# A two-layer decoder trunk in float32 on one core: second products of Strassen pairs accumulated in PSUM, FoX probabilities normalised at the output's gate

## The chip, the core and the metric

The kernel runs on one core of one Trainium2 chip. TensorE (PE) multiplies matrices into PSUM; VectorE (DVE), ScalarE (ACT) and GpSimd (POOL) work element by element; SyncE (SP) issues most loads. The engines run side by side and wait for one another through semaphores. The metric is the device time of one execution in microseconds (us); lower is better.

## What is computed

A decoder trunk of two layers for 1024 tokens of 1024 features, all in float32. In each layer one projection of the normalised input `h` feeds three branches: forgetting attention (FoX, 8 heads of 64), differential attention (4 heads) and a short gated convolution. Each branch is multiplied by its own SiLU gate and projected back, and the three are merged by sigmoid gates. Cut to what matters here:

```python
h = _rmsnorm(x, pre_g)
p = h @ w_in
(fq, fk, fv, ff, fg, dq, dk, dv, dg, cb, cc, cx, cg, mg) = _split_cols(p)
...
    logits = logits + c[:, :, s0:s1, None] - c[:, :, None, :s1]
    p = jax.nn.softmax(jnp.where(_causal_mask(s0, s1), logits, -jnp.inf), axis=-1)
    outs.append(jnp.einsum('bhqk,bhkd->bhqd', p.astype(v.dtype), v[:, :, :s1]))
...
y_fox = y_fox * jax.nn.silu(fg)
y_diff = y_diff * jax.nn.silu(dg)
y_conv = cb * _short_conv(cc * cx, conv_w)
y_conv = y_conv * jax.nn.silu(cg)
gates = jax.nn.sigmoid(mg + b_m).reshape(b, s, N_BRANCH, D_MODEL)
m = (gates[:, :, 0] * (y_fox @ w_fox)
     + gates[:, :, 1] * (y_diff @ w_diff)
     + gates[:, :, 2] * (y_conv @ w_conv))
return x + _rmsnorm(m @ w_o, post_g)
```

## The kernel before

**Split operands.** A float32 operand is held as two float32r tiles, hi and lo, and a product is lo·hi + hi·lo + hi·hi. `mm3` (L343) issues these three matmuls for each tile of 128 along the summed dimension, at L351, L352 and L353; each goes over 512 columns.

**Strassen pairs.** Two chunks of 128 columns of `w_in` that are used one after the other make a pair, 20 pairs in a layer: 6 for the convolution branch (`conv_pair`), 4 for the merge of that branch (`conv_merge`, where each result is multiplied by one more product, `z`), and 10 for gates that are spilled to DRAM (`gates_spilled`). `strassen` (L483) makes a pair with seven products of 12 matmuls where the plain way takes eight. The weights stand on the left: b11, b21 and b22 are quadrants, t1 to t4 sums of them; on the right stand quadrants of `h` (a11, a12, a22) and sums of them (s1 to s4, made once per layer in `build_s`, L444 to L450). The products come in the order b11·a11, b21·a12, t2·s2, t3·s3, t1·s1, t4·a22, b22·s4, each in a PSUM bank of its own; `bank()` hands the eight banks out in turn. DVE adds them up in SBUF tiles `u` and `v` (L497, L498, L500) and in `total` (L521); `use` takes each of the four results on. In the names of the trace a PSUM bank is S, T, O or F.

**Weights of a pair.** `emit_pair` (L304) makes the split weights of the next pair while PE is at the current one. Two loads bring `wraw`. `put` casts a part to `whi` on ACT (L318) and makes `wlo` on POOL (L319); `sub` (L321) forms t1 to t4 on DVE. The parts lie in four tiles: x (b11, b21), y (t2, t3), z (t1, t4) and b (b22). The pool `ws` has three buffers for each kind of tile, so b takes the buffers that x of the same pair had, x of the next pair those of y, y those of z, and z those of b: the first cast into z waits until the last matmul of b22·s4 is done. The sums t1 to t4 are built in tiles `sw`, of which there are two: t4 overwrites t2, and t3 takes t1's when POOL has read that.

**FoX.** `fox_unit` (L866) works on two blocks of 128 queries of one head at a time. Stage 1 makes negated logits and, in `softmax` (L839), the probabilities: least value per row (L847, DVE), exponential with its row sum (L854, ACT), and `norm`, which takes the reciprocal of the sum (L857) and multiplies the whole row of up to 1024 keys by it (L858, DVE). Stage 2 transposes the probabilities on PE (L174), splits them into `pt` (ACT L821, DVE L822) and multiplies with the values (L893, L894). Stage 1 runs one unit ahead of stage 2. Of each step the program says when it would be due by the class `Clock`, an estimate of PE's time, and `later` puts it into its engine's queue in that order; `need(*done)` puts in what a stage needs before it goes on. Projections of the differential branch are spread between the units; POOL splits their weight tiles at L279.

**Gate of the output.** `y_prep` (L1028) loads the spilled output `o` and its gate `g` for 128 rows, multiplies them (L1038, DVE) and splits the product into `yf` (ACT L1043, POOL L1044). For FoX it runs beside the third of the four differential heads.

Of the kernel before, what the change touches and what calls it, by code (L numbers as in the profile page):

```python
# [11 lines left out]
F32 = mybir.dt.float32  # L12
# [8 lines left out]
S = 1024  # L21
D = 1024
P = 128
# [11 lines left out]
# order of the query blocks (pairs) of a head, and of the FoX heads (pairs)  # L35
G_ORDER = (1, 2, 3, 0)
FOX_ORDER = (2, 3, 0, 1)
# work on the tensor engine that runs beside each attention pair or head
# [12 lines left out]
# weights of the attention's steps when work beside it is spread between them  # L51
W1F, W2F, W1D, W2D = 0.188, 1.324, 0.31, 1.574
# PSUM banks: logits, transposes, outputs, work beside the attention
# [3 lines left out]
def mm_us(n):  # L57
    """Time of a pass of n columns through the tensor engine."""
    return max(n, 128) * 0.000417


class Clock:
    """Estimated time of the tensor engine. What the other engines do after one of its steps is emitted
    when its turn would come, beside later steps, so that no engine's queue waits on an early entry."""
# [57 lines left out]
def interleave(main, main_cost, fill, fill_cost):  # L122
    """Emit the steps of main with those of fill spread evenly between them."""
# [12 lines left out]
class Trunk:  # L136
# [35 lines left out]
    def transpose(self, out, x):  # L172
        """One block of 128 x 128, through the tensor engine."""
        self.nc.tensor.transpose(out, x, self.ident)  # L174
# [88 lines left out]
    def emit_load(self, key, kt, nco, eng):  # L263
        """DMA one weight tile [P, kt*nco] and split it into hi + lo float32r parts."""
# [18 lines left out]
    def load_w(self, key, kt, nco, eng="gpsimd"):  # L283
        """The next weight tile; the loads of the tiles after it are issued ahead of its use."""
# [19 lines left out]
    def emit_pair(self, l, i0, i1):  # L304
        """DMA two 128-column weight chunks, b1j and b2j their upper and lower halves, and form the split
        operands of a Strassen-Winograd step: b11, b21 | b12 - b11 (t1), b21 - t2 (t4) |
        b22 - t1 (t2), b22 - b12 (t3) | b22."""
# [38 lines left out]
    def mm3(self, ps, pairs, start=True, stop=True):  # L346
        """Accumulate the products of split operands: lo*hi + hi*lo + hi*hi for each k tile."""
        nc = self.nc
        n = len(pairs)
        for i, (wh, wl, xh, xl) in enumerate(pairs):  # L350
            nc.tensor.matmul(ps, wl, xh, start=start and i == 0, stop=False)  # L351
            nc.tensor.matmul(ps, wh, xl, start=False, stop=False)  # L352
            nc.tensor.matmul(ps, wh, xh, start=False, stop=stop and i == n - 1)  # L353

    def proj_g(self, w, h):
        """One 128-column chunk of the input projection, transposed, for token half h."""
# [18 lines left out]
    # ------------------------------------------------------------------ norm  # L375
    def rstd(self, ss, scale):
        """(ss * scale + EPS) ** -0.5 per partition."""
# [9 lines left out]
    def hk(self, h, k, o=0, n=512):  # L387
        """Tokens o..o+n of a half of hT, 128-row tile k: hi and lo."""
        return [t[:, k % 2, o:o + n] for t in self.hT[h][k // 2]]

    def norm_rows(self, xs, gB, hT, tb0, step):
        """rmsnorm of blocks of 128 tokens (rows of the tiles xs), transposed and split into hT."""
# [40 lines left out]
    # ------------------------------------------------------------------ Strassen-Winograd  # L433
    def build_s(self, L):
        """Sums of the quadrants of h (tokens x features), split: s1 = a21 + a22, s2 = s1 - a11,
        s3 = a11 - a21, s4 = a12 - s2. a21 itself waits in DRAM meanwhile."""
# [46 lines left out]
    def strassen(self, L, c0, c1, use, uv=None):  # L483
        """Two chunks of the input projection, transposed, with seven products in place of eight.
        use(j, h, x, ps, own): chunk j, token half h is x + ps; x may be overwritten if own."""
# [3 lines left out]
        def product(b, a):  # L489
            ps = self.bank()  # L490
# [821 lines left out]
```

## Time and profile before

| | us |
|---|---|
| median of 3 runs | 2570.14 |
| lowest, highest | 2569.18, 2570.54 |
| span of the profiled execution | 2573.8 |
| PE busy (share of the span) | 2439.4 (95%) |
| DVE busy | 1699.8 (66%) |
| ACT busy | 1109.0 (43%) |
| POOL busy | 838.9 (33%) |

The stages of the two layers lie as follows, in us from the start of the span: convolution pairs and the first two gate pairs 72 to 254 and 1351 to 1534, merge of the convolution to 376 and 1656, gate pairs to 531 and 1812, FoX 585 to 849 and 1865 to 2129, differential attention to 1112 and 2393, then the projections of the branches and the output. A busy time is the sum over the engine's instructions; matmuls are pipelined and overlap in the records, so PE's busy time is an upper reading of its work. "Idle before <- releaser" behind an instruction is the time its engine stood idle ahead of it and what it waited for last.

### The profile page before, as it was taken

To read this page: it belongs to the slowest core of one execution; us is meant where nothing else is said; L and a number is where in the kernel's file an instruction comes from. 1 tells how busy PE (TensorE), PEld (TensorE's weight loads), DVE (VectorE), ACT (ScalarE), POOL (GpSimd) and SP (SyncE) were. 2 spreads that over 40 slices of the span, in tenths; PEclk is the share of its full clock that TensorE was granted. 3 is DMA by queue.
4 is the path that set the end of the run, shared out by engine and by line. 5 is a ranking of instruction groups with operands and counts; after the bars stand their busy time and mean duration, and the time that the engine had idled before them with its cause. 6 is when DMAs were issued, how large, how long until landed. Compare 5 with 4: busy or idle time off the path is not lost. (4 is left out here: it accounts for less than half of the span.)

```text
span 2573.8 us, 35788 instructions
## 1 busy us (share of the span) xinstructions
PE 2439.4 (95%) x13104; PEld 2051.8 (80%) x13104; DVE 1699.8 (66%) x3017; ACT 1109.0 (43%) x2282; POOL 838.9 (33%) x605
## 2 busy tenths in 40 slices
PE   7899999999999999899997999999999999989998
PEld 6677888888978778778976778888888787877798
DVE  6976464447687777767578654344486878777664
ACT  4224333336554554543433232233365545555333
POOL 1566334421112222361025652344211122232600
PEclk9899999999999999999998999999999999999999
DMA  4012223332222222563521122233321222225534
GB/s 167 33 50 95 92 96 111 107 132 70 63 69 68 63 87 64 169 220 129 194 90 41 50 95 89 75 117 130 93 80 53 69 68 75 82 70 186 202 119 180
DMA packets 111808, 260.35 MB, mean 101 GB/s; under 512 B 15744, under 2 KB 40576, under 8 KB 111632
## 3 DMA queue, kind: packets, MB, share of 16 engines
q1 hardware_dynamic: 56304, 183.33, 20.7%
q10 hardware_dynamic: 55328, 74.73, 9.4%
q8 instruction: 104, 1.70, 0.3%
q14 instruction: 72, 0.59, 0.1%
HBM read 183.48 MB, written 55.64 MB: 93 GB/s over the span
## 5 line engine op out<-in xcount | busy, mean ns | idle before, releaser
L279 POOL TENSOR_TENSOR wlo<-wraw,whi 128x1024 fp32r<-128x1024 f32 (+2 forms) x93 | 198.5, 2135 | 628.1 <-ACT whi L276 442.3
L351 PE MATMUL F<-ht,wlo 128*128 128x512 f32 x792 | 331.1, 418 | 0.0
L353 PE MATMUL F<-ht,whi 128*128 128x512 f32 x792 | 318.5, 402 | 0.0
L352 PE MATMUL F<-ht,whi 128*128 128x512 f32 x792 | 317.0, 400 | 0.0
L319 POOL TENSOR_TENSOR wlo<-sw,whi 128x512 fp32r<-128x512 f32 x160 | 224.6, 1414 | 228.6 <-ACT whi L318 203.1
L319 POOL TENSOR_TENSOR wlo<-wraw,whi 128x1024 fp32r<-128x1024 f32 x80 | 159.3, 1992 | 188.1 <-ACT whi L318 187.9
L318 ACT CAST whi<-sw 128x512 fp32r<-128x512 f32 x160 | 96.1, 619 | 245.6 <-DVE sw L321 106.1
L353 PEld LDWEIGHTS F<-ht,whi 128*128 128x128 f32 x792 | 150.8, 190 | 30.6
L276 ACT CAST whi<-wraw 128x1024 fp32r<-128x1024 f32 (+2 forms) x126 | 118.0, 939 | 129.8 <-PE F L353 41.9
L822 DVE TENSOR_TENSOR pt<-T,pt 128x512 fp32r<-128x512 f32 (+1 forms) x240 | 147.4, 632 | 37.4 <-ACT pt L821 35.7
L351 PEld LDWEIGHTS F<-ht,wlo 128*128 128x128 f32 x792 | 152.3, 192 | 24.2
L352 PEld LDWEIGHTS F<-ht,whi 128*128 128x128 f32 x792 | 151.5, 191 | 24.5
L821 ACT CAST pt<-T 128x512 fp32r<-128x512 f32 (+1 forms) x240 | 125.1, 544 | 91.3 <-PE T L174 66.1
L783 PE MATMUL S<-qk,qk 128*128 128x512 f32 (+2 forms) x384 | 141.7, 369 | 23.0 <-ACT p L922 21.1
L174 PE MATMUL T<-ident,p 128*128 128x128 f32 x864 | 135.3, 277 | 11.5 <-DVE p L858 6.6
L922 ACT ACTIVATE p<-S,sm 128x512 f32<-128x512 f32 (+2 forms) x192 | 110.5, 582 | 70.2 <-DVE sm L918 35.4
L916 DVE TENSOR_REDUCE sm<-S 128x1 f32<-128x512 f32 (+2 forms) x192 | 104.5, 551 | 48.5 <-PE S L787 29.6
L784 PE MATMUL S<-qk,sw 128*128 128x512 f32 (+2 forms) x384 | 131.8, 348 | 0.0
L318 ACT CAST whi<-wraw 128x1024 fp32r<-128x1024 f32 x80 | 66.8, 834 | 146.0 <-PE S L353 43.7
L351 PE MATMUL F<-whi,ht 128*128 128x256 f32 (+1 forms) x416 | 121.9, 293 | 4.2 <-DVE vd L373 4.2
L854 ACT ACTIVATE p<-p,sm 128x384 f32<-128x384 f32 (+7 forms) x128 | 99.5, 777 | 54.9 <-DVE sm L847 41.5
L321 DVE TENSOR_TENSOR sw<-wraw,sw 128x512 f32<-128x512 f32 x80 | 69.1, 863 | 81.3 <-POOL wlo L319 80.7
(390 smaller groups left out, 7249.2 us busy)
## 6 DMA issues: line engine op xcount, KB each, us to landing
wraw<-wt SPq DMA_DIRECT2D x128, 512.0 KB
mg<-tmp ACTq DMA_DIRECT2D x64, 256.0 KB
sw<-qk ACTq DMA_DIRECT2D x256, 64.0 KB
g<-mg SPq DMA_DIRECT2D x32, 512.0 KB
wraw<-wo SPq DMA_DIRECT2D x32, 512.0 KB
x<-x SPq DMA_DIRECT2D x24, 512.0 KB
wraw<-wbr SPq DMA_DIRECT2D x48, 256.0 KB
m<-tmp ACTq DMA_DIRECT2D x32, 256.0 KB
```

What stands on the lines that cost most here:

```text
L174: self.nc.tensor.transpose(out, x, self.ident)
L276: nc.scalar.copy(hi, raw)
L279: getattr(nc, eng).tensor_tensor(out=lo, in0=raw, in1=hi.bitcast(F32), op=ALU.subtract)
L318: nc.scalar.copy(w[0][:, o], f)
L319: nc.gpsimd.tensor_tensor(out=w[1][:, o], in0=f, in1=w[0][:, o].bitcast(F32), op=ALU.subtract)
L351: nc.tensor.matmul(ps, wl, xh, start=start and i == 0, stop=False)
L352: nc.tensor.matmul(ps, wh, xl, start=False, stop=False)
L353: nc.tensor.matmul(ps, wh, xh, start=False, stop=stop and i == n - 1)
L783: nc.tensor.matmul(ps[:, :wp], q[:, i * P:(i + 1) * P], k[:, c0:c0 + wp], start=True, stop=False)
L784: nc.tensor.matmul(ps[:, :wp], qsw[:, (i % 2) * P:(i % 2) * P + P], k[:, c0:c0 + wp], start=False, stop=not last)
L821: self.clock.later(0.1, lambda: nc.scalar.copy(hi, T[:, n0:]))
L822: done = self.clock.later(0.6, lambda: nc.vector.tensor_tensor(out=lo, in0=T[:, n0:], in1=hi.bitcast(F32), op=ALU.subtract))
```

## The change

`mm3` gets a flag that lets a product add to a bank that is already in use. In `strassen` the second product of three results goes into the bank of an earlier one: b21·a12 is added to b11·a11, t4·a22 to t3·s3, and b22·s4 to t1·s1. For that the earlier sums must have been read first, so the order of the products becomes b11·a11, t2·s2, t3·s3, t1·s1, b21·a12, t4·a22, b22·s4. Two of DVE's additions go in each pair; `use(0, 0, ...)` now takes the bank itself. A pair takes four PSUM banks in place of seven. The number of matmuls is the same.

In FoX, `norm` keeps only the reciprocal, which goes into a column of the tile `rl` of the head pair; the rows of exponentials stay as they are, and stage 2 needs `exp` in place of `norm`. When the last unit of a head pair is out, `sums_out` transposes `rl` on PE and spills it to `rs` in DRAM. `y_prep` loads each head's reciprocals, broadcast to its 64 rows, into `rb` and multiplies `o` by it on POOL, ahead of the multiplication with the gate: 16 such multiplications of 128x512, and 16 loads.

```diff
-    def mm3(self, ps, pairs, start=True, stop=True):
+    def mm3(self, ps, pairs, start=True, stop=True, more=False):
...
-            nc.tensor.matmul(ps, wl, xh, start=start and i == 0, stop=False)
-            nc.tensor.matmul(ps, wh, xl, start=False, stop=False)
-            nc.tensor.matmul(ps, wh, xh, start=False, stop=stop and i == n - 1)
+            nc.tensor.matmul(ps, wl, xh, start=start and i == 0, stop=False, skip_group_check=more)
+            nc.tensor.matmul(ps, wh, xl, start=False, stop=False, skip_group_check=more)
+            nc.tensor.matmul(ps, wh, xh, start=False, stop=stop and i == n - 1, skip_group_check=more)
...
-        def product(b, a):
-            ps = self.bank()
-            self.mm3(ps, [(w[b][0][:, k], w[b][1][:, k], *(t[:, k % 2] for t in L.a[a][k // 2])) for k in range(4)])
+        def product(b, a, ps=None):
+            more = ps is not None
+            ps = ps or self.bank()
+            self.mm3(ps, [(w[b][0][:, k], w[b][1][:, k], *(t[:, k % 2] for t in L.a[a][k // 2])) for k in range(4)],
+                     not more, True, True)
             return ps

         u, v = uv or (self.tmp(), self.tmp())
-        nc.scalar.copy(u, product("b11", "a11"))
-        use(0, 0, u, product("b21", "a12"), False)
-        nc.vector.tensor_tensor(out=u, in0=u, in1=product("t2", "s2"), op=ALU.add)
-        nc.vector.tensor_tensor(out=v, in0=u, in1=product("t3", "s3"), op=ALU.add)
+        add = lambda o, x, ps: nc.vector.tensor_tensor(out=o, in0=x, in1=ps, op=ALU.add)
+        p1 = product("b11", "a11")
+        nc.scalar.copy(u, p1)
+        p6 = product("t2", "s2")
+        add(u, u, p6)
+        p7 = product("t3", "s3")
+        add(v, u, p7)
         p5 = product("t1", "s1")
-        nc.vector.tensor_tensor(out=u, in0=u, in1=p5, op=ALU.add)
-        use(1, 1, v, p5, False)
-        use(0, 1, v, product("t4", "a22"), True)
-        use(1, 0, u, product("b22", "s4"), True)
+        use(0, 0, None, product("b21", "a12", p1), False)
+        use(1, 1, v, p5, True)
+        use(0, 1, u, product("t4", "a22", p7), False)
+        use(1, 0, u, product("b22", "s4", p5), True)
...
         def norm():
-            nc.vector.reciprocal(out=st[:, 2:3], in_=st[:, 2:3])
-            nc.vector.tensor_scalar(out=pr[:, :n], in0=pr[:, :n], scalar1=st[:, 2:3], scalar2=None, op0=ALU.mult)
+            nc.vector.reciprocal(out=rl, in_=st[:, 2:3])
...
-        later(t, exp)
-        done.append(later(2 * t + 0.2, norm))
+        done.append(later(t, exp))
+        later(2 * t + 0.2, norm)
...
+            if g == G_ORDER[-1] and e == 1:
+                self.clock.later(0.5, lambda: self.sums_out(L, p))
...
+    def sums_out(self, L, p):
+
+        nc = self.nc
+        T = self.pT()
+        self.transpose(T[0:16, 0:P], L.rl[p])
+        r = self.tmp((P, P))
+        nc.scalar.copy(r[0:16], T[0:16, 0:P])
+        nc.scalar.dma_start(L.rs[16 * p:16 * p + 16], r[0:16])
...
+        if kind == "f":
+            rb = self.blk([P, S], F32, "rb")
+            rows = L.rs.rearrange("(h t) q -> h (t q)", t=8)
+            for e in range(2):
+                nc.sync.dma_start(rb[e * 64:e * 64 + 64], rows[2 * c + e:2 * c + e + 1].to_broadcast([64, S]))
...
+            if kind == "f":
+                nc.gpsimd.tensor_tensor(out=o1, in0=o1, in1=rb[:, h * 512:h * 512 + 512], op=ALU.mult)
```

PE's queue, from the last matmuls of b11·a11 of a gate pair on (the same pair in both; `ht_6` and `ht_7` are parts of a12, `s2` those of s2). Before:

```order
L352 MATMUL S_504_2878<-ht_5_110,whi_467_2707 128x512
L353 MATMUL S_504_2878<-ht_4_109,whi_467_2707 128x512
L351 MATMUL T_505_2892<-ht_6_111,wlo_468_2708 128x512
L352 MATMUL T_505_2892<-ht_7_112,whi_467_2707 128x512
L353 MATMUL T_505_2892<-ht_6_111,whi_467_2707 128x512
```

After:

```order
L353 MATMUL T_460_2810<-ht_5_110,whi_426_2644 128x512
L354 MATMUL T_460_2810<-ht_4_109,whi_426_2644 128x512
L352 MATMUL F_461_2824<-s2_99_535,wlo_431_2653 128x512
L353 MATMUL F_461_2824<-s2_100_536,whi_430_2652 128x512
L354 MATMUL F_461_2824<-s2_99_535,whi_430_2652 128x512
```

b21·a12 stood right behind b11·a11, in a bank of its own; now t2·s2 stands there. Where it went is the end of t1·s1 of the same pair (`s1` are parts of s1), after:

```order
L352 MATMUL S_463_2852<-s1_112_570,wlo_433_2657 128x512
L353 MATMUL S_463_2852<-s1_113_571,whi_432_2656 128x512
L354 MATMUL S_463_2852<-s1_112_570,whi_432_2656 128x512
L352 MATMUL T_460_2810<-ht_6_111,wlo_427_2645 128x512
L353 MATMUL T_460_2810<-ht_7_112,whi_426_2644 128x512
```

It goes into `T_460`, the bank of b11·a11, as the fifth product, and t3·s3 has moved from fourth to third.

DVE's queue in FoX, in the first window, from a row's least value (L847 before, L856 after, ISA) to the copy of transposed probabilities. Before:

```order
L847 ISA p_970_5712,sm_972_5718<-S_971_5713,cB_968_5705 128x384
L847 ISA sm_972_5718 128x1
L857 RECIPROCAL sm_966_5697<-sm_966_5697 128x1
L858 TENSOR_SCALAR p_959_5659<-p_959_5659,sm_966_5697 128x256
L857 RECIPROCAL sm_972_5718<-sm_972_5718 128x1
L858 TENSOR_SCALAR p_970_5712<-p_970_5712,sm_972_5718 128x384
L822 TENSOR_TENSOR pt_975_5745<-T_976_5746,pt_975_5745 128x384
```

After:

```order
L856 ISA p_910_5586,sm_912_5592<-S_911_5587,cB_908_5579 128x384
L856 ISA sm_912_5592 128x1
L866 RECIPROCAL rl_759_4749<-sm_905_5570 128x1
L866 RECIPROCAL rl_907_5578<-sm_912_5592 128x1
L830 TENSOR_TENSOR pt_915_5617<-T_916_5618,pt_915_5617 128x384
L856 ISA p_910_5586,sm_918_5641<-S_917_5637,cB_908_5579 128x512
```

The two multiplications of whole rows that stood ahead of the copy are gone, and the reciprocals stay.

## Rows read from the trace of the kernel before

**Rows 1.** The page: busy time of each engine over the span, share, instructions.

```profile
PE 2439.4 (95%) x13104; PEld 2051.8 (80%) x13104; DVE 1699.8 (66%) x3017; ACT 1109.0 (43%) x2282; POOL 838.9 (33%) x605
```

**Rows 2.** Windows: length, busy PE, PEld, DVE, ACT, POOL; PEclk; DMA share; GB/s.

```profile
585.00:849.00 264.00, 252.85 (x1635) 218.11 (x1634) 202.67 (x508) 146.26 (x322) 45.70 (x52) 0.99 0.24 67
1865.00:2129.00 264.00, 251.88 (x1632) 217.54 (x1631) 203.68 (x508) 145.93 (x322) 45.10 (x52) 0.99 0.23 67
395.00:512.00 117.00, 117.00 (x506) 94.96 (x505) 51.56 (x69) 43.76 (x66) 54.11 (x36) 1.00 0.32 108
1500.60:1505.90 5.30, 5.23 (x12) 4.13 (x13) 2.58 (x4) 2.19 (x3) 2.82 (x3) 0.50 0.13 49
```

**Rows 3.** PE's waits: line waited for, us in total, times, longest.

```profile
PE O L893 <- DVE pt L822: 12.6, 8, 2.0
PE O L351 <- POOL wlo L319: 8.6, 1, 8.6
PE T L174 <- DVE p L858: 6.6, 9, 1.7
PE S L351 <- ACT s L448: 5.4, 1, 5.4
PE F L351 <- POOL wlo L319: 5.4, 3, 3.4
PE S L351 <- POOL wlo L319: 5.1, 3, 3.4
PE T L351 <- POOL wlo L319: 4.0, 1, 4.0
```

**Rows 4.** Timeline of a gate pair: start us, us, engine, line, [idle before <-releaser].

```profile
414.86 0.40 PE L351 MATMUL F<-ht,wlo 128*128 128x512 f32 x1
414.27 0.69 DVE L321 TENSOR_TENSOR sw<-wraw,sw 128x512 f32<-128x512 f32 x1 [1.34 <-POOL wlo L319]
415.11 1.14 ACT L318 CAST whi<-sw 128x512 fp32r<-128x512 f32 x2 [1.42 <-PE O L353]
415.81 2.55 POOL L319 TENSOR_TENSOR wlo<-sw,whi 128x512 fp32r<-128x512 f32 x2 [1.57 <-ACT whi L318]
417.14 1.77 DVE L321 TENSOR_TENSOR sw<-wraw 128x512 f32<-128x512 f32 x1 [1.40 <-POOL wlo L319]
419.64 1.29 POOL L319 TENSOR_TENSOR wlo<-sw,whi 128x512 fp32r<-128x512 f32 x1 [1.28 <-ACT whi L318]
423.19 0.40 PE L351 MATMUL F<-s,wlo 128*128 128x512 f32 x1
```

**Rows 5.** Timeline, two convolution pairs: t3's low part and its product.

```profile
136.02 1.30 POOL L319 TENSOR_TENSOR wlo<-sw,whi 128x512 fp32r<-128x512 f32 x1 [2.48 <-ACT whi L318]
137.73 0.40 PE L351 MATMUL O<-s,wlo 128*128 128x512 f32 x1
...
1414.53 1.76 POOL L319 TENSOR_TENSOR wlo<-sw,whi 128x512 fp32r<-128x512 f32 x1 [1.28 <-ACT whi L318]
1417.57 0.40 PE L351 MATMUL S<-s,wlo 128*128 128x512 f32 x1
```

**Rows 6.** Timeline, the gate pair with the least slack: the same two.

```profile
518.09 1.30 POOL L319 TENSOR_TENSOR wlo<-sw,whi 128x512 fp32r<-128x512 f32 x1 [1.28 <-ACT whi L318]
520.74 0.40 PE L351 MATMUL T<-s,wlo 128*128 128x512 f32 x1
```

**Rows 7.** Timeline of PE behind a wait in a convolution pair.

```profile
1500.67 0.79 PE L351 MATMUL S<-s,wlo 128*128 128x512 f32 x1 [3.44 <-POOL wlo L319]
```

**Rows 8.** Groups of instructions on DVE: count, busy us, mean ns, idle before.

```profile
L858 DVE TENSOR_SCALAR p<-p,sm 128x384 f32<-128x384 f32 (+7 forms) x128 | 89.7, 702 | 3.4
```

**Rows 9.** Timeline of DVE in FoX, beside POOL's L279 and without.

```profile
708.63 2.14 DVE L858 TENSOR_SCALAR p<-p,sm 128x384 f32<-128x384 f32 x1
...
768.48 0.42 DVE L858 TENSOR_SCALAR p<-p,sm 128x384 f32<-128x384 f32 x1
```

**Rows 10.** Timeline of POOL beside `y_prep`: the low part of `yf`.

```profile
1049.78 1.29 POOL L1044 TENSOR_TENSOR yf<-o,yf 128x512 fp32r<-128x512 f32 x1 [14.45 <-ACT yf L1043]
```

More of the change, by code (lines that the diff above doesn't have):

```diff
@@ L593, in use @@
             sl = slice(h * 512, h * 512 + 512)
-            y = self.total(x, ps, own)
+            s = self.total(x, ps, own)
+            y = self.tmp() if x is None else s
             i = l * 24 + 16 + dc + j
-            nc.scalar.activation(y, y, AF.Sigmoid, bias=self.par[:, i:i + 1])
+            nc.scalar.activation(y, s, AF.Sigmoid, bias=self.par[:, i:i + 1])
             z = self.bank()
@@ L609, in use @@
             name, c = (a, b)[j]
-            y = self.total(x, ps, own)
+            s = self.total(x, ps, own)
+            y = self.tmp() if x is None else s
             if name == "mg":
-                nc.scalar.activation(y, y, AF.Sigmoid, bias=self.par[:, l * 24 + c:l * 24 + c + 1])
+                nc.scalar.activation(y, s, AF.Sigmoid, bias=self.par[:, l * 24 + c:l * 24 + c + 1])
             else:
                 sg = self.tmp()
-                nc.scalar.activation(sg, y, AF.Sigmoid)
-                nc.vector.tensor_tensor(out=y, in0=sg, in1=y, op=ALU.mult)
+                nc.scalar.activation(sg, s, AF.Sigmoid)
+                nc.vector.tensor_tensor(out=y, in0=sg, in1=s, op=ALU.mult)
             nc.scalar.dma_start(L.g[name][c, :, h * 512:h * 512 + 512], y)
@@ L837, in pv_group, with softmax @@
         return po
-    def softmax(self, chunks, n, pr, cb, done):
+    def softmax(self, chunks, n, pr, cb, rl, done):
         nc, later = self.nc, self.clock.later
@@ L873, in stage1 @@
             hd = 2 * p + e
+            if g == G_ORDER[0] and e == 0:
+                L.rl[p] = self.sm(16, "rl")
             if g == G_ORDER[0]:
@@ L883, in stage1 @@
                 chunks, n = self.logits(q, qsw, k, i)
-                self.softmax(chunks, n, pr, cb, done)
+                self.softmax(chunks, n, pr, cb, L.rl[p][:, 8 * e + i:8 * e + i + 1], done)
                 yield W1F * (i + 1)
@@ L1134, in layer @@
         L.c = dt([8, S], "c")
+        L.rs, L.rl = dt([64, P], "rs"), {}
         L.g = {"fg": dt([4, P, S], "fg"), "dg": dt([4, P, S], "dg"), "mg": dt([16, P, S], "mg")}
```

## The prediction

> **What bounds the kernel now.** The page's first part comes first: TensorE (PE) is busy for 2439.4 us of 2573.8, 95%, and VectorE (DVE) for 66% [rows 1]. So a shorter DVE step pays only where PE stands waiting for it, and a step that makes PE wait costs its full length. The two parts of the change touch different stages, so each is read in its own.
>
> Windows come next [rows 2]. In the gate pairs (395 to 512 us) PE has no idle time at all: the Strassen steps there run at the rate of the matmuls, and DVE works 51.56 of 117 us. In the two FoX windows (264 us each) PE is idle for 11.15 and 12.12 us while DVE is busy for 203 and 204. DVE work that is removed can pay in FoX; in the gate pairs it cannot.
>
> Then PE's waits [rows 3]. In FoX it waits 12.6 us (8 times) for DVE's `pt` at L822 and 6.6 us (9 times) for DVE's `p` at L858. In the Strassen steps it waits for the low weight parts `wlo` that GpSimd (POOL) makes at L319: 8.6 + 5.4 + 5.1 + 4.0 = 23.1 us, 8 times in 7 pairs, and once 5.4 us for `s` from L448. These waits show that the weight preparation, not the sums after the products, is what can hold PE up in a Strassen step.
>
> Last, the timeline of a steady pair [rows 4]. At 414.86 the last product of the pair before (b22·s4) has ended and b11·a11 starts; three products later, at 423.19, t3·s3 starts, so a product of 12 matmuls takes 2.78 us, 0.23 us for each. Only the end of b22·s4 lets ACT cast t1 and t4 of the new pair (415.11), since z takes the tiles that b22 held. POOL makes their low parts (415.81, 2.55 us). DVE may form t3 = b22 − b12 when t1's buffer is free again (417.14); it takes 1.77 us where another L321 subtraction of the same width takes 0.69, because POOL is at work beside it. Then come the cast and t3's low part on POOL, ready at 419.64 + 1.29 = 420.93. That is 6.07 us after b22·s4 ended. PE wants it at 423.19: the slack is 2.26 us.
>
> **The change, part by part.**
>
> *Order of the products.* Before, t3·s3 is the fourth product; after, b21·a12 stands behind t1·s1, and t3·s3 is the third. PE asks for t3's low part 5.56 us after the end of b22·s4, and the chain that makes it keeps its 6.07 us: the cast waits for the same matmul, and no instruction of the chain changes. So one product of cover, 2.78 us, is gone from the slack of every pair, and a wait of 0.05 us more than the shortfall (the time from POOL's end to the matmul in a wait) takes its place. By pairs, of 40:
> - Seven pairs already wait for L319 [rows 3], and the very first waits for `s`. There the moved product stood ahead of the wait and now stands behind it: 8 × 2.78 = 22.2 us.
> - Four pairs in the convolution stages just miss a wait [rows 5]. In the first, the low part is ready at 136.02 + 1.30 = 137.32 and its product starts at 137.73; two more are alike, and the fourth has 1.28 us (1416.29 against 1417.57). 3 × (2.78 − 0.40 + 0.05) + (2.78 − 1.28 + 0.05) = 8.9 us.
> - Seventeen pairs have the slack of [rows 4], or come to the same (the first merge pair of each layer also loses the cover of its first `z` product): 17 × (2.78 − 2.26 + 0.05), with a few at 2.33, is 8.9 us. Four more have 1.35 to 2.00 us, the tightest in [rows 6] (519.39 against 520.74): 4.6 us together.
> - Seven pairs at or behind a merge pair keep a `z` product between, and over 2 us of slack: nothing.
>
> Sum: 44.6 us. The other weight tiles keep room: x is now held for longer, and b22, which takes x's tiles in the same pair, is cast after the fifth product and not the second, for the seventh; one product (2.78 us) lies between, against a cast and a low part of 0.6 and 1.29 us, with t1 and t4 already made.
>
> *Clock.* After the 3.44 us wait at 1500.67 [rows 7] the granted clock is 0.50, the 1.2 GHz level, and 12 matmuls take 5.28 us and not 2.78 [rows 2]: 2.5 us more. Three waits of 1 to 1.5 us grow past that length: 3 × 2.5 = 7.5 us. The bounds are 0 and 15, the last if the three new waits of 2.4 us bring it too.
>
> *Fewer additions.* Two DVE additions per pair go, 80 in all at about 0.69 us [rows 4]. They lie beside PE's matmuls, and PE waits for none of them: nothing. The three sums in PSUM need no more matmuls, and a bank is written again only one product or more after its reader could start, against a reader of 0.7 us: nothing.
>
> *Normalisation.* 128 multiplications at L858 go, 89.7 us of DVE, mean 0.70 us [rows 8]. One of 384 columns takes 0.42 us alone and 2.14 us while POOL splits a weight tile [rows 9], and right behind that long one DVE has the `pt` copy (L822) that PE waits for. So the `pt` waits and the `p` waits are both of L858's making where it is long: 12.6 + 6.6 = 19.2 us in 17 waits. Each is short by 0.17 us in the table, since a matmul's record is 0.40 us long and the next normally follows after 0.23: 2.9 us. The clock of 0.99 in both windows [rows 2] is 2.6 us at half rate in each, 1.3 us lost, 2.6 in all. That makes 24.7; the transposes now wait for ACT's exponential itself, so some of it stays, and I take 23. The bounds are 6.6 (only the waits on `p`) and 29 (all 23.3 us idle in [rows 2], with both additions).
>
> The rows show POOL and DVE holding each other up, 0.42 against 2.14 us. The Trainium skill, "SBUF — State Buffer", section "Who interferes with whom", states why: the two share one pair of ports under an exclusive lock, which a tensor_scalar between SBUF tiles or an operation with two SBUF inputs takes, and the later of the two blocks for the whole instruction. By that rule L858 is worth removing, but the multiplications that the change puts on POOL can each block a DVE step in the differential stage. By the rows alone I take 2 us for that, below; by that rule it would be nearer the 10 of rival C, and the sum +40.
>
> *The division moved to `y_prep`.* 16 multiplications of 128x512 on POOL, bounded by the 1.29 us of the low part of the same size [rows 10]: 20.6 us of POOL. POOL stood idle for 14.45 us ahead of one such step, so most of it is hidden. If the cover were gone, the whole chain to `yf` would be late by it. Behind a blocked DVE stands the softmax that PE needs. Bounds 0 and 10 (half of it), I take 2. The 16 broadcast loads on SP stand ahead of the gate's load; nothing near waits for them. Eight transposes, copies and stores of 16 rows: 0.5 us, on PE alone.
>
> Sum: 44.6 + 7.5 + 2 + 0.5 − 23 = +31.6 us. On the profiled 2573.8 that is 2605.4. The median of the runs, 2570.14, lies 3.7 us under that execution's span, so **2602 us**.
>
> **Rivals.**
> - *A, faster.* The weight preparation hides after all: t3's low part is ready within 5.56 us of the end of b22·s4, and the conv pairs' waits shrink because DVE has fewer additions ahead of the next pair's subtractions. For it: 0.5 us is all that is missing in a steady pair. Against it: the chain is four steps on three engines, none of which the change shortens. Strassen then costs 5, FoX gives 29: −24, **2546**. It decides by whether PE still runs without idle time in the gate pairs.
> - *B, balance.* Only the blocked subtraction moves: t3's DVE step gets in ahead of POOL and takes 0.69 instead of 1.77 us, so the chain is 5.0 us. The steady pairs then wait nothing, four give 0.8, near misses 4.6, the rest 22.2: 27.6, clock 2.5, `y_prep` and transposes 2.5, FoX −29: +4, **2574**.
> - *C, larger loss.* The 2.4 us waits bring the half clock too (15), `y_prep` blocks DVE for 10 us, and FoX gives only 15 since its transposes wait for ACT: 44.6 + 15 + 10 + 0.5 − 15 = +55, **2625**. It decides by whether a POOL multiplication and a DVE step of the softmax fall together, as in [rows 9]; ACT's exponential stood right ahead of L858. The rule of the Trainium skill on the shared ports speaks for it.
>
> **How the numbers follow.** 0.2% is 5.1 us, about what a measurement of this kernel can tell from no change. Forecast 0.66 (own range 2588 to 2616), A 0.12, B 0.12, C 0.10. B lies half within the limit and half beside it: faster 0.13, same 0.08, slower 0.79. The range leaves out A and the outer part of C: 2562 to 2630.
>
> **What would show it.** In the gate windows PE shows a wait of about 0.5 us on L319's `wlo` ahead of each t3·s3; the total of PE's waits on it rises from 23 to some 65 us. In FoX PE's wait on `pt` L822 falls below 4 us. In `y_prep` no DVE step is over 2 us. Wrong would be: gate pairs still without PE idle time (A), t3's subtraction at 0.69 us (B), or new PE waits on the exponential at the transposes (C).

## The result

The changed kernel takes 2591.25 us (median of 4 runs, 2590.08 to 2598.72) where the kernel before takes 2569.94 in the same comparison: a ratio of 1.0087, 95% interval 1.007 to 1.0104, 21 us slower. The profiled execution has a span of 2589.1 us, 15.2 more than that of before. The forecast was 2602, with a range of 2562 to 2630.

The page's first part, as in [rows 1]: DVE has 133 us less to do, and the time is longer all the same.

```profile
PE 2443.1 (94%) x13112; PEld 2047.6 (79%) x13112; DVE 1567.2 (61%) x2815; ACT 1104.6 (43%) x2290; POOL 843.3 (33%) x615
```

Windows as in [rows 2]: the same six gate pairs, which are now 4 us longer, and the two FoX stages, 15 and 13.5 us shorter than before.

```profile
416.40:537.40 121.00, 118.69 (x505) 94.39 (x505) 44.52 (x57) 42.74 (x66) 53.02 (x36) 1.00 0.29 103
608.00:857.00 249.00, 248.10 (x1639) 217.57 (x1637) 162.98 (x444) 146.89 (x325) 45.53 (x52) 1.00 0.25 71
1885.00:2135.50 250.50, 248.45 (x1638) 217.63 (x1636) 163.12 (x444) 146.49 (x325) 45.59 (x52) 1.00 0.25 71
```

PE had no idle time in the gate pairs and has 2.3 us now. In FoX it was idle for 11.15 and 12.12 us and is for 0.90 and 2.05. PE's waits, as in [rows 3] (line waited for, us, times, longest):

```profile
PE T L352 <- POOL wlo L319: 31.1, 17, 10.3
...
PE F L352 <- POOL wlo L319: 12.0, 7, 5.2
...
PE S L352 <- POOL wlo L319: 6.5, 8, 3.1
...
PE T L352 <- DVE uv L498: 1.9, 1, 1.9
...
PE O L903 <- DVE pt L830: 1.2, 1, 1.2
```

The waits on L319 were 23.1 us, 8 times; they are 49.6 us, 32 times. FoX's wait on `pt` fell from 12.6 to 1.2 us, and the wait on L858 is gone with the line.

Where the time went, by stage, for all kernels of this study. Each number is the length of a stage in the profiled execution less its length in the kernel before; the stages end at the last block of the input norm, the last matmul with a sum s in a Strassen pair, the first and the last product of FoX's probabilities with the values, and the first product that projects the differential branch back, as the traces have their starts. "Between" is the projections ahead of FoX, "diff." differential attention with `y_prep` beside it.

| kernel | Strassen, layer 0 / 1 | between | FoX | diff. | rest | span |
|---|---|---|---|---|---|---|
| changed | +26.2 / +13.2 | −2.9 / −2.8 | −15.1 / −14.0 | +3.6 / +8.9 | −1.9 | +15.2 |
| e1_strassen | +26.3 / +13.0 | −2.9 / −2.9 | −2.4 / 0.0 | −0.9 / +0.3 | −0.5 | +30.0 |
| e2_fox | −2.7 / −1.3 | −1.5 / −1.6 | −15.1 / −14.5 | +5.8 / +5.6 | −1.9 | −27.2 |
| e3_t1first | +2.1 / −2.4 | −2.9 / −2.8 | −14.4 / −14.8 | +3.4 / +4.4 | −1.1 | −28.5 |
| e4_nodiv | +25.8 / +13.0 | −2.9 / −2.8 | −14.9 / −12.1 | +1.2 / +2.0 | −0.3 | +8.9 |
| e5_reuse | +4.8 / −2.2 | −2.9 / −2.8 | −14.9 / −14.6 | +7.0 / +7.8 | −1.0 | −18.8 |
| e6_latemul | +2.1 / +0.1 | −2.9 / −2.8 | −15.1 / −14.3 | −0.4 / +2.1 | −2.2 | −33.4 |
| e7_t3early | −0.4 / −7.0 | −2.9 / −2.8 | −15.0 / −15.4 | +8.7 / +9.2 | −2.8 | −28.3 |
| e8_all | +1.6 / +2.6 | −2.8 / −3.0 | −15.0 / −14.8 | +8.5 / +5.5 | −5.3 | −22.7 |
| e9_best | +1.1 / −5.4 | −2.9 / −2.8 | −14.3 / −15.5 | +2.6 / +4.0 | 0.0 | −33.1 |
| e10_ownbanks | −7.8 / −11.5 | −1.6 / 0.0 | −14.4 / −15.5 | +0.8 / +1.4 | −1.6 | −50.3 |

So the change is the sum of a loss in Strassen (39.4 us), a gain in FoX (29.1), a loss beside `y_prep` (12.5), and some 7.6 us of gain that no term had: 5.7 between the gates and FoX, the rest small. How far a stage can be read shows in e2_fox: its Strassen code is that of the kernel before, and its Strassen stages are 4.0 us shorter. Each row is one execution: that of before lies 3.7 us above its median, those of e3_t1first and e9_best 8 us below and 6 us above theirs.

A steady gate pair of the changed kernel, as in [rows 4]:

```profile
436.64 0.40 PE L352 MATMUL T<-ht,wlo 128*128 128x512 f32 x1
...
437.59 2.54 POOL L319 TENSOR_TENSOR wlo<-sw,whi 128x512 fp32r<-128x512 f32 x2 [1.56 <-ACT whi L318]
...
438.93 1.76 DVE L321 TENSOR_TENSOR sw<-wraw 128x512 f32<-128x512 f32 x1 [1.40 <-POOL wlo L319]
...
441.41 1.28 POOL L319 TENSOR_TENSOR wlo<-sw,whi 128x512 fp32r<-128x512 f32 x1 [1.28 <-ACT whi L318]
...
442.75 0.50 PE L352 MATMUL F<-s,wlo 128*128 128x512 f32 x1 [0.36 <-POOL wlo L319]
```

The chain is what it was: t3's low part is ready at 442.69, 6.05 us after the end of b22·s4 at 436.64. PE stands before t3·s3 until then.

The same loss by pairs, from the last matmul of a pair to the last of the next (for the first pair of a layer from the last block of the input norm), less the kernel before:

| pairs of 40 | forecast | changed | e2_fox | e3_t1first | e7_t3early | e9_best | e10_ownbanks |
|---|---|---|---|---|---|---|---|
| first of layer 0 / 1 | +2.8 / +2.8 | +10.7 / +5.0 | −0.4 / +0.2 | +8.0 / +8.9 | +7.8 / +5.9 | +7.8 / +5.9 | −0.9 / −0.3 |
| six others that waited for L319 before | +24.2 with the clock | +4.6 | −3.8 | −17.7 | −21.4 | −18.4 | −18.4 |
| the four near misses | +8.9 | +5.7 | 0.0 | +0.1 | +0.1 | +0.1 | +0.3 |
| the other 28 | +13.5 | +13.4 | 0.0 | +0.4 | +0.3 | +0.3 | 0.0 |

The last two rows show the lost cover of t3 by itself: it costs there in the changed kernel alone, and nothing where t3 is asked for later (e3) or made earlier (e7, e9). The first pairs are another matter: they lose 14 to 17 us together in every accumulating kernel of this table, also where t3 costs nothing, and about nothing in e2 and e10, which have the old order and a bank for each product. In layer 0 PE waits for parts of `s` in both kernels, in the kernel before:

```profile
84.13 0.80 PE L351 MATMUL F<-s,wlo 128*128 128x512 f32 x1 [4.12 <-ACT s L448]
...
97.84 0.80 PE L351 MATMUL S<-s,wlo 128*128 128x512 f32 x1 [5.44 <-ACT s L448]
```

([Rows 3] show only the second of these.) In the changed kernel PE has ten of the twelve matmuls of the next pair's b11·a11 in its queue ahead of t4·a22, and waits there for the low part of b11 too (3.6 and 3.7 us in e3, e7 and e9, not at all in e2 and e10):

```profile
83.78 0.79 PE L352 MATMUL O<-s,wlo 128*128 128x512 f32 x1 [6.86 <-ACT s L449]
...
96.40 0.65 PE L352 MATMUL F<-s,wlo 128*128 128x512 f32 x1 [3.31 <-ACT s L449]
...
105.65 3.45 POOL L319 TENSOR_TENSOR wlo<-wraw,whi 128x1024 fp32r<-128x1024 f32 x1 [3.42 <-ACT whi L318]
109.15 0.79 PE L352 MATMUL T<-ht,wlo 128*128 128x512 f32 x1 [4.66 <-POOL wlo L319]
```

### The profile page after: what moved, and what is told of

It is laid out like the page before. It is cut to its first block, busy times and chain, and to the rows that moved or that the text cites. A ratio compares the mean times of both kernels' runs of the same rounds, so it can differ in the third digit from the quotient of the medians.

```text
span 2589.1 us, 35593 instructions
## 1 busy us (share of the span) xinstructions
PE 2443.1 (94%) x13112; PEld 2047.6 (79%) x13112; DVE 1567.2 (61%) x2815; ACT 1104.6 (43%) x2290; POOL 843.3 (33%) x615
## 5 line engine op out<-in xcount | busy, mean ns | idle before, releaser
L279 POOL TENSOR_TENSOR wlo<-wraw,whi 128x1024 fp32r<-128x1024 f32 (+2 forms) x93 | 200.8, 2161 | 590.6 <-ACT whi L276 424.0
L352 PE MATMUL F<-ht,wlo 128*128 128x512 f32 x816 | 339.2, 416 | 0.0
L353 PE MATMUL F<-ht,whi 128*128 128x512 f32 x816 | 326.2, 400 | 0.0
L354 PE MATMUL F<-ht,whi 128*128 128x512 f32 x816 | 326.0, 399 | 0.0
L319 POOL TENSOR_TENSOR wlo<-sw,whi 128x512 fp32r<-128x512 f32 x160 | 223.8, 1410 | 172.5 <-ACT whi L318 142.5
L319 POOL TENSOR_TENSOR wlo<-wraw,whi 128x1024 fp32r<-128x1024 f32 x80 | 152.0, 1900 | 320.2 <-ACT whi L318 320.2
L354 PEld LDWEIGHTS F<-ht,whi 128*128 128x128 f32 x816 | 154.5, 189 | 32.2
L353 PEld LDWEIGHTS F<-ht,whi 128*128 128x128 f32 x816 | 155.5, 191 | 26.0
L174 PE MATMUL T<-ident,p 128*128 128x128 f32 x864 | 130.1, 275 | 3.4 <-DVE p L954 3.2
L352 PE MATMUL F<-whi,ht 128*128 128x256 f32 (+1 forms) x416 | 123.0, 296 | 3.9 <-DVE vd L374 3.9
L354 PE MATMUL F<-whi,ht 128*128 128x256 f32 (+1 forms) x416 | 117.3, 282 | 0.0
```

The source lines that it names most:

```text
L279: getattr(nc, eng).tensor_tensor(out=lo, in0=raw, in1=hi.bitcast(F32), op=ALU.subtract)
L319: nc.gpsimd.tensor_tensor(out=w[1][:, o], in0=f, in1=w[0][:, o].bitcast(F32), op=ALU.subtract)
L353: nc.tensor.matmul(ps, wh, xl, start=False, stop=False, skip_group_check=more)
```

## The experiments

### The two parts apart

**e1_strassen** is the changed kernel with FoX as before:

```diff
-            nc.vector.reciprocal(out=rl, in_=st[:, 2:3])
+            nc.vector.reciprocal(out=st[:, 2:3], in_=st[:, 2:3])
+            nc.vector.tensor_scalar(out=pr[:, :n], in0=pr[:, :n], scalar1=st[:, 2:3], scalar2=None, op0=ALU.mult)
...
-        done.append(later(t, exp))
-        later(2 * t + 0.2, norm)
+        later(t, exp)
+        done.append(later(2 * t + 0.2, norm))
```

and without `sums_out`, `rb` and its multiplication.

> The changed kernel with the FoX part undone: probabilities are normalised row by row again, and only the Strassen pairs accumulate in PSUM. Theory (t3's low part loses the cover of one product): the Strassen stages cost what they do in the changed kernel, 39 us, and nothing else moves: 2570 + 39 = 2609 us, with PE waiting about 0.6 us on L319 ahead of each t3·s3 of the gate pairs. Rival (the two parts disturb each other, the Strassen part alone is cheap): 2570 to 2585 us.

Measured: 2608.33 us against 2572.26, ratio 1.014 (1.0125 to 1.0155), 36 us slower.

**e2_fox** is the changed kernel with the products of `strassen` as before (the removed lines of the diff put back).

> The changed kernel with the Strassen part undone: products in the old order, each in its own bank, additions on DVE; FoX probabilities stay unnormalised until the gate. Theory: FoX gives 29 us, the stretch beside y_prep takes back 11, the projections around gain some 6: 2570 - 24 = 2546 us. Rival (FoX gained only because it began later, behind other loads): under 10 us of gain, over 2560 us.

Measured: 2550.5 us, ratio 0.9913 (0.9898 to 0.9928), 22 us faster. Stage by stage the two parts add to within some 4 us, and beside `y_prep` the layers differ (3.6 and 8.9 in the changed kernel, 5.8 and 5.6 in e2). The totals add less well: by the medians 36 less 22 is 14 us, where the changed kernel has 21, and by the spans 30.0 less 27.2 is 2.8 and not 15.2, in part since the long execution of before is subtracted twice. A loss of some us that only the two together bring is not excluded. Both rivals fall.

### Is it the place of t3·s3?

**e3_t1first** swaps two products:

```diff
-        p7 = product("t3", "s3")
-        add(v, u, p7)
         p5 = product("t1", "s1")
+        p7 = product("t3", "s3")
+        add(v, u, p7)
```

> The changed kernel with one change: t1·s1 is the third product and t3·s3 the fourth, so that PE asks for t3's low part 8.3 us after the end of b22·s4 again, and not 5.6; accumulation, banks and number of instructions stay. Theory (the lost product of cover): PE's waits on L319 go back to some 23 us and the gate pairs have no idle PE; the 39 us go but for the first pair of a layer (2 times 2.8): 2591 - 34 = 2557 us, or less if the 80 additions that are gone help the convolution pairs. Rival (the accumulation itself costs, by PE waiting for readers of a bank, or by the later use of b21·a12): 2580 us or more.

Measured: 2554.79 us, ratio 0.9933 (0.9916 to 0.9949); as a ratio to before, 1.5% under the changed kernel, some 39 us. Strassen's loss went from 39.4 us to −0.3. PE in the six gate pairs again has no idle time:

```profile
397.50:514.70 117.20, 117.20 (x505) 94.84 (x504) 44.54 (x57) 42.77 (x66) 53.14 (x36) 1.00 0.32 106
```

The accumulation is the same here and the number of instructions too; so the loss of the changed kernel in Strassen hangs on asking for t3's low part one product earlier. That the sum comes out at zero is partly chance: the first pairs cost 16.9 us here too, and the six pairs that waited give 17.7 back. With t3·s3 as the fourth product, only b21·a12 stands between writing its bank and adding t4·a22 to it, and in the first pair of layer 1 PE waits for DVE to have read the bank:

```profile
1370.44 0.79 PE L352 MATMUL F<-ht,wlo 128*128 128x512 f32 x1 [9.14 <-DVE uv L498]
```

**e7_t3early** comes from the other side: it keeps the changed order, and shortens the chain of t3.

```diff
-            tc.tile_pool(name="swaps", bufs=2) as swaps,
+            tc.tile_pool(name="swaps", bufs=3) as swaps,
...
-        z = new()
-        put(z, u, t1)
         t3 = self.sw()
         sub(t3, fb[:, d], fb[:, u])
         sub(t2, fa[:, d], t2)
         put(y, d, t3)
+        z = new()
+        put(z, u, t1)
         put(z, d, t2)
```

> The changed kernel with its order of products, but a third buffer for the sums t1 to t4, and t3's cast and low part put ahead of t1's: t3's chain no longer waits for b22's tiles or for POOL's t1. Theory (the chain of t3's low part is what PE waits for): ready about 1 us after the end of b22·s4 and wanted at 5.6, so the gate pairs have no idle PE, and the convolution pairs lose most of the 23 us that they wait in the kernel before as well: 2591 - 39 - 10 = 2542 us. Rival (it is the order of the products or the accumulation that costs): over 2580 us.

Measured: 2547.36 us against 2571.28, ratio 0.9908 (0.9894 to 0.9922). Gate pairs without idle PE:

```profile
393.60:510.80 117.20, 117.20 (x506) 94.93 (x505) 44.11 (x57) 43.36 (x66) 53.74 (x37) 1.00 0.30 107
```

PE's waits in e7:

```profile
PE O L352 <- ACT s L449: 8.6, 1, 8.6
PE T L352 <- ACT s L449: 8.3, 1, 8.3
...
PE T L352 <- DVE uv L498: 5.2, 2, 3.1
...
PE T L352 <- POOL wlo L319: 3.7, 1, 3.7
...
PE F L352 <- DVE uv L498: 3.1, 2, 2.0
```

Waits on L319 are down from 49.6 to 3.7 us. Strassen stands at −7.4 us against the kernel before, near the −10 expected; the rest of what is missing lies beside `y_prep` (+17.9 us, for 12.5 in the changed kernel). PE now waits for `s`, and 8.3 us for DVE's addition L498. That last wait belongs to the accumulation: a product may go into a bank only when the bank's earlier sum has been read, and in the convolution pairs DVE comes to that addition late.

### What the division at the gate costs

**e4_nodiv** leaves out the multiplication and the loads:

```diff
-            rb = self.blk([P, S], F32, "rb")
-            rows = L.rs.rearrange("(h t) q -> h (t q)", t=8)
-            for e in range(2):
-                nc.sync.dma_start(rb[e * 64:e * 64 + 64], rows[2 * c + e:2 * c + e + 1].to_broadcast([64, S]))
...
-                nc.gpsimd.tensor_tensor(out=o1, in0=o1, in1=rb[:, h * 512:h * 512 + 512], op=ALU.mult)
```

> The changed kernel without the division in y_prep: the 16 multiplications on POOL and the 16 broadcast loads are left out, so FoX's output stays unnormalised. Theory (POOL's multiplication waits for its load, and the gate's multiplication behind it holds DVE up): the stretch beside y_prep loses nothing, 11 us less: 2580 us, and the time from the first product of differential attention to the last is as before. Rival (the stretch is late because FoX finished earlier and other work fell into it): 2588 us or more.

Measured: 2584.32 us, ratio 1.0042 (1.0026 to 1.0058), where the changed kernel has 1.0087: 0.45%, some 11 us. The stretch loses 3.2 us in both layers together and not 12.5.

In the changed kernel the trace shows the wait. DVE, ahead of the gate's multiplication (L1066), POOL's (L1065), and the product behind it in stage 2 of differential attention:

```profile
1077.87 2.54 POOL L1065 TENSOR_TENSOR o<-o,rb 128x512 f32<-128x512 f32 x2 [0.67 <-DMA rb<-rs]
...
1079.98 1.57 DVE L1066 TENSOR_TENSOR o<-o,g 128x512 f32<-128x512 f32 x2 [5.21 <-POOL o L1065]
...
1086.42 0.57 PE L985 MATMUL O<-pt,vd 128*128 128x256 f32 x1 [1.70 <-DVE pt L830]
```

DVE stands idle for 5.21 us with the softmax queued behind L1066. Most of that is POOL's queue: it is at the low part of the chunk before until 1077.20, which itself stood 5.15 us behind ACT. Then 0.67 us are left to wait for the load. That load is issued late: `o` at 1065.62, its `rb` from 1069.75 on. SP waits 3.7 and 3.2 us ahead of the two parts of `rb`, by the trace for transfers of ACT's queue; that these hold the block which the load needs is argued.

```profile
1074.65 2.55 POOL L1072 TENSOR_TENSOR yf<-o,yf 128x512 fp32r<-128x512 f32 x2 [5.15 <-ACT yf L1071]
...
1065.62 0.33 SPq L1053 DMA_DIRECT2D o<-of  x1
1069.75 4.13 SPq L1058 DMA_DIRECT2D rb<-rs  x2
```

Over the whole execution POOL waits for `rb` 27.8 us in 5 places, and DVE for POOL's product 11.7 us in 2.

**e5_reuse**, on top of e3_t1first, gives `rb` the tile of the low part instead of a block of its own:

```diff
+        y = [self.blk([P, S], F32R, f"y{kind}") for _ in range(2)]
         if kind == "f":
-            rb = self.blk([P, S], F32, "rb")
+            rb = y[1].bitcast(F32)
...
-        y = [self.blk([P, S], F32R, f"y{kind}") for _ in range(2)]
```

> The kernel of e3_t1first, with the reciprocals loaded into the tile that takes the low part of the product later, so that y_prep needs four blocks for a chunk again and not five; all instructions stay. Theory (the load of rb waits on SP for a free block, and POOL, then DVE, wait for the load): the stretch beside y_prep gets back some 7 of its 11 us: 0.3% under e3_t1first. Rival (POOL's multiplications as such hold DVE up, by 1.3 us each): no change from e3_t1first.

Measured: 2555.12 us, ratio 0.9934 (0.992 to 0.9949), no different from e3 (0.9933). The edit did not do what it was for. The low part's tile is a block too, and it must be free earlier now, so the load that DVE's wait hangs on still comes 5.1 us behind that of its `o` (4.1 in the changed kernel), and DVE waits as before:

```profile
1045.63 0.33 SPq L1053 DMA_DIRECT2D o<-of  x1
1050.70 4.20 SPq L1059 DMA_DIRECT2D yf<-rs  x2
```

```profile
DVE o L1066 <- POOL o L1065: 5.4, 1, 5.4
```

What the load costs as such stays open.

**e6_latemul**, also on top of e3_t1first, moves what stands behind POOL's multiplication:

```diff
-            later(0.0, mul)
+            dt = 4.0 if kind == "f" else 0.0
+            later(dt, mul)
...
-            later(1.0, lambda o1=o1, hi=hi: nc.scalar.copy(hi, o1))
+            later(dt + 1.0, lambda o1=o1, hi=hi: nc.scalar.copy(hi, o1))
```

(and the sigmoid and the low part alike).

> The kernel of e3_t1first, with the gate's multiplication on DVE, the cast and the low part of FoX's y_prep put into their queues 4 us later by the program's clock; POOL's multiplication and all loads stay where they are. Theory (the gate's multiplication stands at the head of DVE's queue while POOL waits for its load): DVE's wait of 5.2 us on POOL's o goes, and 3 to 7 us of the stretch with it: 0.1 to 0.3% under e3_t1first. Rival (the wait only moves to the products of yf): no change.

Measured: 2541.66 us, ratio 0.9886 (0.987 to 0.9901), 0.47% under e3, some 12 us, more than the 3 to 7 expected. The stretch beside `y_prep` costs −0.4 and +2.1 us where e3 has +3.4 and +4.4, and DVE's wait on POOL's `o` is gone. (The profiled execution of e3 is its shortest, 8 us under its median; by the spans the difference is 5.) POOL still makes all 16 multiplications, and the delay gives back as much as leaving them out did (e4, 11 us from the changed kernel): so they cost little as such, and what hurts is a queue whose head waits for them. How little is not settled. The 1.7 us that the stretch loses were measured at a granted clock of 0.99, where the kernel before had 0.97 and 0.98 (e6, third from the right):

```profile
833.15:1135.15 302.00, 280.74 (x1531) 230.15 (x1530) 232.93 (x477) 159.72 (x402) 119.62 (x98) 0.99 0.40 128
2093.40:2397.30 303.90, 280.63 (x1530) 229.87 (x1529) 233.36 (x477) 159.89 (x402) 120.03 (x99) 0.99 0.40 128
```

The edit also moves ACT's cast and POOL's low part, so DVE's queue is not told apart from theirs.

### Together, and what accumulation is worth

**e8_all** adds to e7 the edit of e5 and, for the first pair of a layer, the old place of b21·a12:

```diff
+        first, L.begun = not hasattr(L, "begun"), True
+        if first:
+            use(0, 0, u, product("b21", "a12"), False)
         p6 = product("t2", "s2")
...
-        use(0, 0, None, product("b21", "a12", p1), False)
+        if not first:
+            use(0, 0, None, product("b21", "a12", p1), False)
```

> e7_t3early with two more edits: the reciprocals in the tile of the low part (as in e5_reuse), and in the first pair of each layer b21·a12 as the second product in a bank of its own, as before the change, since PE waits there for s. Theory: 7 us from y_prep and 2 times 2.8 us from the first pairs, on top of e7_t3early: 2530 us. If the first pairs wait for something else behind s, or y_prep for POOL itself, under 4 us less than e7_t3early.

Measured: 2551.98 us, ratio 0.9928 (0.9914 to 0.9941), against 0.9908 for e7: nothing gained, and Strassen is 2.0 and 9.6 us longer than in e7. PE, in the first pairs of layer 1:

```profile
1360.60 0.80 PE L352 MATMUL S<-s,wlo 128*128 128x512 f32 x1 [6.92 <-ACT s L449]
...
1376.01 0.80 PE L352 MATMUL S<-ht,wlo 128*128 128x512 f32 x1 [6.48 <-DVE uv L498]
```

The wait for `s` is shorter than e7's 8.3 us, but then a product stands 6.48 us before its bank, until DVE has added the earlier sum. With b21·a12 taken out from between, only one product is left between writing the bank and adding to it.

**e9_best** is e7 with e6's edit of `y_prep`.

> e7_t3early and e6_latemul together: the changed kernel with a third buffer for the sums, t3's split ahead of t1's, and the gate's multiplication of FoX's y_prep put into DVE's queue 4 us later. If the two losses are independent, as the theory says: e7_t3early's 2547 less the 18 us that its stretch beside y_prep takes above the 2 that stay: 2530 us. If the wait of y_prep only moves: 2545 us.

Measured: 2536.66 us against 2570.79, ratio 0.9871 (0.9858 to 0.9885). That is 7 us over the theory and under the rival. The stretch beside `y_prep` falls from +17.9 in e7 to +6.6 us, both layers together.

**e10_ownbanks** is e9 with `strassen` as in the kernel before: the old order, a bank for each product, the 80 additions back on DVE.

> e9_best with the Strassen products in the old order and each in its own bank again (the 80 additions on DVE are back); the third buffer, t3's early split, FoX and y_prep stay. Tells what accumulating in PSUM is worth once t3 is early. Theory (PE does not wait for the additions; accumulating puts b21·a12 behind the wait for s in the first pairs, 2 times 2.8 us, and makes PE wait for the reader of a bank, 8 us by e7_t3early's profile): 10 us less than e9_best, 2520 us. Rival (the 80 additions fewer on DVE help the weights of the convolution pairs): 5 us or more above e9_best.

Measured: 2525.7 us, ratio 0.9827 (0.9813 to 0.984), 45 us faster than before and 11 us faster than e9. In the Strassen stages it is 15 us shorter than e9 (−7.8 and −11.5 against +1.1 and −5.4), by the spans 17 us in all, since e9's profiled execution is its longest. By the table of pairs the first pairs alone make 15.0 us, and the rest cancels. PE's waits there:

```profile
PE O L352 <- ACT s L449: 8.2, 1, 8.2
...
PE F L352 <- ACT s L449: 5.8, 1, 5.8
...
PE S L352 <- ACT s L449: 4.5, 1, 4.5
```

No wait on an addition is left. So accumulation in PSUM with the order of products that it needs, the first half of the change, is worth less than nothing on this kernel even when t3 is early. Which of the two costs the time, the order or the shared banks, no run tells apart. e10 is the fastest kernel of the study: FoX normalised at the gate, the gate's multiplication later, and t3's split early.

## Why the prediction was right

The direction, the two places and the mechanism of the steady pairs held; the time was 11 us under the forecast. By the spans +31.6 us was worked out and +15.2 came: Strassen was put 12.7 us too high, FoX's gain 6.1 too low, 7.6 us of gain had no term, and the division was put 10 us too low. That the errors partly cancel is luck. (The median of the changed kernel lies 2.1 us above its profiled span, where that of before lay 3.7 below.)

- **Order of the products.** The chain of 6.07 us against a demand at 5.56 is what the trace shows (6.05), and e3 and e7 show it by cutting either end. Strassen with its clock term was put at 52.1 us and measured 39.4. The pairs that wait in steady state come out as said: the six gate pairs are 4.0 us longer, 0.66 us each, against 0.57, and the 28 pairs of the last row of the table by pairs 13.4, against 13.5. The step that failed is the one product of 2.78 us for each of eight waiting pairs: with the clock they were put at 29.7 us and cost 20.3, and not by 2.78 each. The two first pairs took 15.7, most of it in layer 0, where a third wait came and the granted clock fell from 0.81 (72.60 to 108.83 us) to 0.74 (72.60 to 119.20). The other six took only 4.6, because waits of the kernel before went as well: the 4.0 us in [rows 3] stood in the second pair of layer 1, which is now 6.5 us shorter. Too large were the near misses as well: by the distance from one pair's start to the next, the four of [rows 5] cost 1.7, 1.2, 1.7 and 1.1 us, 5.7 together and not 8.9, because there the low part was ready earlier in its pair than before (7.1 us after b22·s4 and not 7.9 in the first). Two fewer additions ahead of it on DVE would do that, as rival A had it: in four of the pairs that waited for L319 before, the second and the seventh of each layer, e9 is 7.6 us shorter than e10. But no run takes the additions away alone.
- **Clock.** 7.5 us were for three waits of 1 to 1.5 us that grow past 3.44. One of the three was 0.76 us and grew to 3.13, and PE stayed at full clock behind it; the other two, of 1.20, brought a stretch of lower clock that cost about 1.5 us each: pairs that grew by 4.3 us, of which 2.8 are the product. Behind a wait of 3.13 us, then behind two of 4 us, the windows (granted clock third from the right):

```profile
125.70:128.60 2.90, 2.87 (x12) 2.36 (x13) 1.82 (x3) 0.00 (x0) 0.00 (x0) 1.00 0.00 0
190.90:194.20 3.30, 3.30 (x10) 2.68 (x11) 3.30 (x5) 0.00 (x0) 0.00 (x0) 0.69 0.00 0
...
1468.40:1471.50 3.10, 3.10 (x8) 2.49 (x9) 3.10 (x5) 0.00 (x0) 0.00 (x0) 0.56 0.00 0
```

  The step that failed is taking the price of one wait, [rows 7], for every wait of that length: in e2, with the Strassen code of before, a wait of 3.43 us cost no clock where the same wait of before did (last section).
- **Fewer additions, and the banks.** That "a bank is written again only one product or more after its reader could start" and costs nothing was wrong by 1.9 us in the changed kernel, by 8.3 in e7, 9.1 at one place in e3 and 6.5 at one in e8. The reader's own 0.7 us were counted, and not what DVE has queued ahead of it in the convolution pairs.
- **Normalisation.** 23 us were forecast, 29.1 measured, the upper bound. Of the waits in [rows 3] for `pt` and `p` 1.2 us stayed, and the stretches at half clock went with them (the windows stand at 1.00). By the windows PE's idle time fell by 20.3 us and its busy time by 8.2. The step that failed is holding some back for the exponential, 1.7 us: no wait on it at the transposes came. The clock was misread as well: 0.99 over 264 us is 2.6 us lost in each window, as far as two digits tell, and not 1.3. What makes the rest of the 6.1 us is not broken down.
- **The division.** 2 us were taken, at most 10, and 9 to 11 came (e4). The mechanism was not the one that the upper bound was made of. POOL's 20.6 us were mostly hidden; the price is a queue that stands behind a multiplication, which itself comes late by POOL's own queue and by a load. The prediction named the loads on SP and said that nothing near waits for them: that sentence is the one that was wrong, by POOL's 27.8 us.
- **Not in the sum:** 2.8 us less in each layer between the gates and FoX. It comes with the Strassen part (e1 has it, e2 only half). There PE waits for a DVE step, L677 before and L685 after, and the granted clock of the stretch rose from 0.97 to 1.00 in both layers (531.60 to 593.20 us before, 557.50 to 616.20 after, in layer 0). The wait is 3.2 us in every kernel that accumulates, and 5.9 and 5.8 in e2 and e10; that the fewer additions on DVE shorten it was not tried. Before, then after:

```profile
PE S L686 <- DVE tmp L677: 5.8, 2, 2.9
...
PE S L694 <- DVE tmp L685: 3.2, 2, 1.6
```

- **The rivals.** A and B fall by the gate pairs: PE waits there, and t3's subtraction still takes 1.76 us. C's price beside `y_prep` came true, by another mechanism than the one it named, and the rest of C did not.
- **The signs.** The waits ahead of t3·s3 and FoX's `pt` came as named. PE's waits on L319 rose to 49.6 us and not to some 65. DVE steps over 2 us do stand beside `y_prep`, as 2.74 us at 1041.81 (L707), but beside POOL's L279 and not beside its multiplication.

The rule that the Trainium skill, "SBUF — State Buffer", gives in "Who interferes with whom" was weighed for the multiplications on POOL; by it they were put nearer 10 us than 2. The trace agrees that DVE is held up beside them (the last section has a row). But e6 gives back as much with all of the multiplications in place as e4 without them, so the block costs little here, and most of the 9 to 11 us that came has another cause.

## What to carry to other kernels

When products are reordered so that a sum can be made in PSUM, count for each moved product what it was covering: here one product of 2.78 us hid the last 0.5 us of a weight's preparation in most pairs, and moving it cost more than the additions that it saved were worth, which PE did not wait for. A product that is added to a bank also waits for whoever reads the bank's earlier sum, and for all that the reader has queued ahead: see that more than one product stands between, and look at the first steps of a stage by themselves, where other things are late as well. Work that leaves a busy engine pays where the trace shows that the bottleneck stands behind it (here L858), and a step that waits for another engine belongs into its queue only when that engine can be done. Where two kernels differ by a gain and a loss in different stages, a table by stage finds both in one reading, and each half can be kept or dropped by itself.

## What was not expected of the hardware

- Waits of the same or nearly the same length on PE left its clock at different levels. The waits stand in brackets in PE's timeline below, and the windows behind them stand under the clock's point above. After 3.13 us the granted clock was 1.00, after 3.97 it was 0.69, after 3.96 it was 0.56, and before the change 3.44 us brought 0.50 [rows 2, 7].

```profile
125.73 0.50 PE L352 MATMUL S<-s,wlo 128*128 128x512 f32 x1 [3.13 <-POOL wlo L319]
...
190.90 0.50 PE L352 MATMUL F<-s,wlo 128*128 128x512 f32 x1 [3.97 <-POOL wlo L319]
...
1468.40 0.53 PE L352 MATMUL T<-s,wlo 128*128 128x512 f32 x1 [3.96 <-POOL wlo L319]
```

  e2 has the Strassen code of before, and in the same pair a wait of the same 3.43 us. Behind it the granted clock was 1.00 and 14 matmuls ran in 3.30 us, where before it was 0.50 and 8 ran. The length of a wait alone does not say what it costs. (In layer 1 the 3.44 us of [rows 7] stand in e2 too, and brought 0.54.) The wait and the window of e2, then the window of before:

```profile
220.10 0.50 PE L352 MATMUL F<-s,wlo 128*128 128x512 f32 x1 [3.43 <-POOL wlo L319]
220.10:223.40 3.30, 3.30 (x14) 2.71 (x15) 2.76 (x5) 2.00 (x3) 0.87 (x1) 1.00 0.00 0
...
220.80:224.10 3.30, 3.29 (x8) 2.62 (x9) 2.57 (x4) 1.98 (x3) 0.85 (x1) 0.50 0.00 0
```

- In the changed kernel a DVE step of a single column took 1.03 us while POOL ran L1065; the median of the 64 steps of this line is 0.159 us. In this row the time lost beside POOL is not in proportion to the step that is held up. The timeline:

```profile
1056.40 2.54 POOL L1065 TENSOR_TENSOR o<-o,rb 128x512 f32<-128x512 f32 x2 [10.70 <-DMA rb<-rs]
1056.67 1.03 DVE L953 TENSOR_TENSOR sm<-sm,nlam 128x1 f32<-128x1 f32 x1
```

All steps of the line (ns, least/median/most, first and last start):

```profile
L953 DVE TENSOR_TENSOR sm<-sm,nlam x64: 142/159/1320, 858.9 to 2404.3; 128x1 f32<-128x1 f32 x64
```
